# The first feed-forward product of blocks two to four by seven products, its weight sums made in block one, and the last norm off VectorE

## The chip, the cores and the metric

The kernel runs on one core of a Trainium2 chip. A core has five engines that run their own instruction streams: TensorE (PE, matmul, with a separate weight load), VectorE (DVE), ScalarE (ACT), GpSimd (POOL) and SyncE (SP), which here only issues DMAs. The metric is the device time of one execution in microseconds (us); it was measured three times for the kernel before.

## The reference

One decoder layer in fp32 over 2048 tokens of width 1024: a gated DeltaNet mixer of 8 heads and a memory cross-attention of 4 heads share one input projection and one output projection; then a post-norm, a feed-forward network and a second post-norm. The part that the change touches:

```python
D_MODEL = 1024; SEQ = 2048; D_FF = 4 * D_MODEL; ALPHA = 2.0 ** 0.25
def layer_norm(x, g, b):
    mu = x.mean(-1, keepdims=True)
    var = jnp.square(x - mu).mean(-1, keepdims=True)
    return (x - mu) * lax.rsqrt(var + LN_EPS) * g + b
def sqrelu_mlp(x, w1, w2):
    return jnp.square(jax.nn.relu(x @ w1)) @ w2
...
mix = gdn_mixer(x, mem_k, mem_v, ...)
x = layer_norm(ALPHA * x + mix, ln1_g, ln1_b)
x = layer_norm(ALPHA * x + sqrelu_mlp(x, w_ff1, w_ff2), ln2_g, ln2_b)
```

## The kernel before

**Blocks and stages.** The 2048 tokens run in four blocks of 512 (`TB`), one after the other; the recurrent state is carried between them. In a block follow: input projections (`aq`, `ak`, `av`, `az`), the gates and the chunked delta rule by heads, the output projection (`ao`, summed into the token tiles `y`, 128 tokens by 1024 each), norm 1, the two feed-forward products (FF1 and FF2, both in PSUM banks named `af` in the profile), norm 2 and the store.

**Precision.** Each fp32 operand is split into a high part (an ACT cast) and a low part (a DVE subtraction), and `mm3` (L475) makes each product by three matmuls: high x high, high x low, low x high. For a weight tile of 128x1024 this is one DMA into `wraw`, one cast and one subtraction into a `whl` pair. There are `NW` = 4 `whl` pairs and `NR` = 3 `wraw` buffers (L387). The transposed tokens after norm 1 lie in `Thi` and `Tlo`, made by `to_T` (L535): eight transposes of 128x128 per token tile into `pt` and two splits.

**FF1** (`ff1_tiles`, L1213) makes one 128-feature tile by 512 tokens with `project` (L548): 8 contraction tiles of 128, 24 matmuls of 512 columns. The first four tiles of a block run in two token halves of 256 columns instead, so that PE can begin before the last token tiles are through norm 1. `relu2` (L1208) squares the positive part on ACT.

**FF2** (`ff_seven`, L1011) runs in 4 groups `g` of 1024 features, each of two parts `v`. It uses the Winograd form of Strassen's product: seven products of halves in place of eight, with sums `S1` to `S4` of the left operand (`ss4` tiles on DVE, from the squares `sq2`; both show as `ss` and `sq`) and sums of the weights, which `keep_sums` (L991) makes on DVE in block 1 and stores in DRAM as `tsc`. The table `SEVEN` lists the products and the banks that they are added into.

**Last norm.** `layer_norm` (L512) takes statistics and their aggregate on DVE (`bn`, `mv`), two tiny POOL steps (`ve`, `rs`), and then per half of 512 columns two DVE steps with g and b; norm 2 of a block runs in the middle of FF2's last group and behind it, together with the first projections and the gates (`gab`, `gp`, `gg`, then `pg`, `pgt` on PE) of the next block, which `next_block` (L1115) sets in between.

**Order.** No engine's order is written by hand. Every operation is recorded, and `Recorder.issue` simulates the five engines with a cost per operation (`cost`), latencies and buffer releases, and takes on each engine the ready operation of the smallest recorded index plus `nc.shift`. The resulting order is fixed at build time; the hardware then only waits by semaphores. All instructions are issued at L330, so in the profile one goes by the tiles' names. All DMAs stand in SP's queue, in order.

Of the kernel before, what the change touches and what calls it, by code (L numbers as in the profile page):

```python
# [14 lines left out]
P = 128  # L15
TB = 512
# [330 lines left out]
def hybrid_layer(  # L347
# [102 lines left out]
    inv = {}  # L450
    for n, f in (("LB", P), ("XB", P), ("L32", P), ("X32", P), ("X64", P), ("L64", P), ("Q", 64)):
        inv[n] = rec.buf(cst, (P, 2, f), F32, n, 1, n)
        nc.gpsimd.memset(inv[n], 0.0)
# [58 lines left out]
    def layer_norm(y, g, b, dst=None):  # L512
        st = small("bn", [P, 2, BN_DIM])
        for i in range(2):
            nc.vector.bn_stats(out=st[:, i], in_=y[:, i * 512:(i + 1) * 512].part(i))
        mv = small("mv", [P, 2])
        nc.vector.bn_aggr(out=mv, in_=st)
        ve = small("ve", [P, 1])
        nc.gpsimd.tensor_scalar_add(ve, mv[:, 1:2], LN_EPS)
        rs = small("rs", [P, 1])  # L520
        nc.gpsimd.tensor_tensor(out=rs, in0=ve, in1=mhalf[:, 0:1], op=ALU.pow)
        for i in range(2):
            c = slice(i * 512, (i + 1) * 512)
            yi = y[:, c].part(i)
            nc.vector.scalar_tensor_tensor(out=yi, in0=yi, scalar=mv[:, 0:1], in1=g[:, c],
                                           op0=ALU.subtract, op1=ALU.mult)
# [17 lines left out]
    def T_tiles():  # L544
        return (rec.buf(tp, (P, KT, TB), F32R, "Thi", 1, "Thi"),
                rec.buf(tp, (P, KT, TB), F32R, "Tlo", 1, "Tlo"))

# [458 lines left out]

    SEVEN = (("A11", "B11", "A", False, (0, 0)), ("S3", 3, "C", False, (1, 1)), ("S2", 2, "A", True, (1, 0)),
# [3 lines left out]
    def ff_seven(b, ff1_tiles, relu2, add, norm2):  # L1011
        Q = 2 * P
        for g in range(NS):
# [3 lines left out]
            for v in range(2):  # L1017
                lo = [slot("xl", "s%d" % v, F32R) for _ in range(7)]
                hi = [slot("xh", "d", F32R) for _ in range(7 if v == 0 else 4)]
                if v:  # L1020
                    hi += [hq[:, 0].part(0), hq[:, 1].part(1), slot("xh", "on", F32R)]
                sqs = [None, None]
                fs = [8 * g + 2 * v + o for o in (0, 4, 1, 5)]
                for part in ((0, 1, 2, 3),) if g == 0 and v == 0 else ((0,), (1,), (2,), (3,)):
                    if b == 0:
                        for j in range(2):
                            if 2 * j in part:
                                keep_sums(u0 + v, j)
                    for i, a in zip(part, ff1_tiles([fs[i] for i in part], len(part) > 1)):
# [7 lines left out]
                        st = tok_tile("ss4")  # L1037
                        a11, a21, a12, a22 = (sq[:, q * Q:(q + 1) * Q] for q in range(4))
                        s = [st[:, q * Q:(q + 1) * Q].part(q // 2) for q in range(4)]
                        sub = lambda o, x, y, op=ALU.subtract: nc.vector.tensor_tensor(out=o, in0=x, in1=y, op=op)  # L1040
                        sub(s[0], a21, a22, ALU.add)
                        sub(s[1], s[0], a11)
                        sub(s[2], a11, a21)
                        sub(s[3], a12, s[1])
                        h3, l3 = hi[3 * j:3 * j + 3], lo[3 * j:3 * j + 3]
                        two = lambda ap: ap.rearrange("p (i f) -> p i f", i=2)
                        split(sq.rearrange("p (j i f) -> p i j f", j=2, i=2)[:, 0], two(h3[0]), two(l3[0]))
                        h22 = hi[6][:, j * Q:(j + 1) * Q].part(("x", j))
                        l22 = lo[6][:, j * Q:(j + 1) * Q].part(j)
                        split(a22, h22, l22)  # L1050
                        for q in range(2):
                            split(st[:, q * TB:(q + 1) * TB].part(q), h3[1 + q], l3[1 + q])
                        x = {"A22": (h22, l22)}
                        for q, (n0, n1) in enumerate((("A11", "A12"), ("S1", "S2"), ("S3", "S4"))):
                            x[n0] = h3[q][:, :Q], l3[q][:, :Q]
                            x[n1] = h3[q][:, Q:], l3[q][:, Q:]
                        X[2 * v + j] = x
# [57 lines left out]
    def next_block(b, step):  # L1115
# [3 lines left out]
        if step < 4:  # L1119
# [3 lines left out]
            xj = rec.buf(wp, (P, 1024), F32, "wraw", NR, "xj").rearrange("p (k f) -> p k f", k=2)  # L1123
# [8 lines left out]
    for b in range(NB):  # L1132
# [12 lines left out]
        for i in range(12):  # L1145
            cat_slot(i)
        r, A = {}, {}
# [14 lines left out]
        def out_proj(k0, tail=None):  # L1162
# [28 lines left out]
            else:  # L1191
                for t in range(NC):
# [8 lines left out]
        T1 = T_tiles()  # L1201

        def norm1(t):
            layer_norm(ys[t], g1, b1)
            to_T(ys[t], T1[0], T1[1], t)

# [6 lines left out]
        def ff1_tiles(fs, halves):  # L1213

            wa = [(load_cols(w_ff1, f), bank("af", "m" if halves and i == 3 else "acc")) for i, f in enumerate(fs)]
            for t0, n in ((0, 256), (256, 256)) if halves else ((0, TB),):
                for w, a in wa:
                    project(a[:, t0:t0 + n], w, T1, n, t0)
            return [a for _, a in wa]

# [12 lines left out]
        ff_seven(b, ff1_tiles, relu2, add, norm2)  # L1233
# [56 lines left out]
```

## Time and profile before

| what | value |
|---|---|
| time, median of 3 runs | 2924.38 us (2924.02 to 2924.44) |
| the profiled execution | 2924.22 us |
| its span | 2922.5 us |
| mean granted TensorE clock | 0.994 of full speed |
| PE, DVE, ACT, POOL busy in the feed-forward of block 2 (301 us) | 300.0, 184.3, 148.8, 2.0 us |
| the same at the transition to block 3 (46 us) | 42.2, 40.6, 15.7, 9.5 us |

The span is the profiler's, from the first to the last instruction; the time holds a little more. In the profile a row of a group reads: engine, operation, output and inputs, shapes, count, then busy us and mean ns of one, then the idle time just ahead of such instructions and what ended it. In a timeline a row begins with start and length in us; a wait stands in brackets with its releaser. Matmuls overlap, so the pace of a row of matmuls, not the length of one, is what it costs.

### The profile page before, as it was taken

The numbers are of one execution on the slowest core, as the hardware profiler recorded it, in microseconds if no ns is written. First come the engines' busy times: TensorE is split into PE (matmuls) and PEld (weight loads), VectorE is DVE, ScalarE is ACT, GpSimd is POOL, SyncE is SP. The second block draws the span as 40 slices with busy tenths as digits, with TensorE's granted clock in tenths as the row PEclk, the third lists the DMA queues.
The fourth block names the chain that finished last, engine by engine and source line by source line (L and its number), as shares of the span: only waits on it lengthen the run. The fifth ranks groups of instructions, "written<-read, shape, count | busy, mean of one in ns | idle before, by whom it ended". The sixth has DMA issues, their size and how long they took to land.

```text
span 2922.5 us, 42803 instructions
## 1 busy us (share of the span) xinstructions
PE 2863.8 (98%) x14404; PEld 2387.9 (82%) x14404; DVE 2182.8 (75%) x5762; ACT 1528.2 (52%) x3678; POOL 419.6 (14%) x1033
## 2 busy tenths in 40 slices
PE   8999999999999999999999999999999999999998
PEld 6888778888788888888878888888877888888886
DVE  7999987666788886665578887756667888676667
ACT  6677625554356652555436665344454666444443
POOL 1334200000123311000013331100002223010000
PEclk9999999999999999999999999999999999999999
DMA  7755567655743322544474333244446332324444
GB/s 254 271 202 202 175 207 249 204 188 187 265 166 127 125 96 80 159 139 136 151 261 146 138 109 105 87 151 144 151 161 245 139 139 95 104 94 147 149 144 137
DMA packets 127708, 469.79 MB, mean 161 GB/s; under 512 B 14464, under 2 KB 16896, under 8 KB 109056
## 3 DMA queue, kind: packets, MB, share of 16 engines
q1 hardware_dynamic: 126912, 467.00, 47.6%
q8 instruction: 114, 1.87, 0.3%
q14 instruction: 106, 0.87, 0.1%
q10 hardware_dynamic: 576, 0.06, 0.0%
HBM read 402.97 MB, written 64.03 MB: 160 GB/s over the span
## 4 chain that ended last, share of the span: by engine, by line
PE 84%; DVE 12%; issue 1%; POOL 1%; ACT 1%; DMA 0%; POOLq 0%; ACTq 0%; DVEq 0%
PE af L330 43%; PE ao L330 7%; PE aq L330 5%; PE az L330 4%; PE ak L330 4%; PE av L330 4%; PE pc L330 3%; PE amq L330 3%; DVE y L330 3%; PE po L330 2%; PE pkq L330 1%; PE pq L330 1%; PE pp L330 1%; DVE bn L330 1%; DVE whl L330 1%
## 5 line engine op out<-in xcount | busy, mean ns | idle before, releaser
L330 DVE TENSOR_TENSOR whl<-wraw,whl 128x1024 fp32r<-128x1024 f32 (+1 forms) x446 | 540.1, 1217 | 424.2 <-ACT whl L330 414.9
L330 PE MATMUL af<-Thi,whl 128*128 128x512 f32 (+1 forms) x2304 | 650.7, 367 | 7.0 <-DVE whl L330 6.4
L330 ACT CAST whl<-wraw 128x1024 fp32r<-128x1024 f32 (+1 forms) x446 | 466.4, 1047 | 359.8 <-PE af L330 196.2
L330 PEld LDWEIGHTS af<-Thi,whl 128*128 128x128 f32 x2304 | 417.7, 189 | 78.5 <-DVE whl L330 7.2
L330 PE MATMUL af<-whl,xh 128*128 128x512 f32 x1536 | 473.6, 390 | 3.1 <-DVE whl L330 3.1
L330 PE MATMUL af<-Tlo,whl 128*128 128x512 f32 (+1 forms) x1152 | 422.0, 366 | 0.0
L330 PE MATMUL af<-whl,xl 128*128 128x512 f32 x896 | 346.1, 389 | 0.0
L330 PEld LDWEIGHTS af<-whl,xh 128*128 128x128 f32 x1536 | 287.7, 188 | 66.5 <-DVE whl L330 5.0
L330 PE MATMUL ao<-whl,ch 128*128 128x512 f32 x768 | 254.2, 402 | 2.0 <-DVE y L330 1.6
L330 PEld LDWEIGHTS af<-Tlo,whl 128*128 128x128 f32 x1152 | 217.9, 189 | 34.9
L330 POOL TENSOR_SCALAR ve<-mv 128x1 f32<-128x1 f32 x34 | 24.9, 731 | 1512.7 <-DVE mv L330 1487.1
L330 ACT ACTIVATE rl<-af 128x512 f32<-128x512 f32 x128 | 76.5, 598 | 274.0 <-PE af L330 272.1
L330 PEld LDWEIGHTS af<-whl,xl 128*128 128x128 f32 x896 | 168.2, 188 | 34.9
L330 PE MATMUL aq<-Thi,whl 128*128 128x512 f32 x512 | 179.5, 410 | 8.4 <-ACT Thi L330 6.9
L330 PE MATMUL av<-Thi,whl 128*128 128x512 f32 x512 | 181.2, 413 | 0.0
L330 DVE SCALAR_TENSOR_TENSOR y<-y,af 128x512 f32<-128x512 f32 x224 | 148.8, 683 | 43.2 <-PE af L330 43.2
L330 PE MATMUL ak<-Thi,whl 128*128 128x512 f32 x512 | 173.7, 402 | 0.0
L330 PE MATMUL az<-Thi,whl 128*128 128x512 f32 x512 | 171.8, 401 | 0.1
L330 PEld LDWEIGHTS ao<-whl,ch 128*128 128x128 f32 x768 | 142.5, 188 | 28.6 <-DVE y L330 2.9
L330 PE MATMUL ao<-whl,cl 128*128 128x512 f32 x384 | 152.3, 399 | 0.0
L330 PEld LDWEIGHTS aq<-Thi,whl 128*128 128x128 f32 x512 | 95.4, 191 | 24.4 <-ACT Thi L330 6.9
L330 PEld LDWEIGHTS av<-Thi,whl 128*128 128x128 f32 x512 | 97.7, 195 | 16.5
(257 smaller groups left out, 5812.8 us busy)
## 6 DMA issues: line engine op xcount, KB each, us to landing
wraw<-in_w_ff_dram SPq DMA_DIRECT2D x224, 512.0 KB, 4.1
whl<-wsc SPq DMA_DIRECT2D x108, 1024.0 KB, 4.9
wraw<-tsc SPq DMA_DIRECT2D x128, 512.0 KB, 3.4
wsc<-whl SPq DMA_DIRECT2D x36, 1024.0 KB, 5.6
wraw<-in_w_out_dram SPq DMA_DIRECT2D x48, 512.0 KB, 3.9
wraw<-in_w_in_dram SPq DMA_DIRECT2D x35, 512.0 KB, 6.5
wq<-in_w_ff_dram SPq DMA_DIRECT2D x64, 256.0 KB, 4.4
tsc<-wq SPq DMA_DIRECT2D x64, 256.0 KB, 3.8
```

The source lines that it names most:

```text
L330: o.fn(*[res(a) for a in o.args], **{k: res(v) for k, v in o.kw.items()})
```

## The change

1. FF1 of blocks 2 to 4 is made by seven products as well: the contraction (1024) is halved, the 256-feature output and the 512 tokens are halved, and each product is 24 matmuls of 256 columns for each of two 128-feature tiles (`FF1_SEVEN`, `ff1_quads`). Block 1 keeps `ff1_tiles`.
2. The weight sums `S1` to `S4` that this needs are made by POOL in block 1 from the raw FF1 weights (`ff1_sums`) and stored in DRAM as `fsc`: 128 sums and 128 stores of 128x256. The raw weights keep their `wraw` buffers until then.
3. The transposed tokens are kept as quadrants (`quad_tiles`, `to_quads`): four plain or summed quadrants in `Thi`/`Tlo`, the sums T1, T2, T4 in other tiles' places, T1 in a `whl` pair. The token tiles go through the last output projection in the order 2, 3, 0, 1, since the sums need both halves of the tokens.
4. Reading the results: ACT copies and squares of 256 columns, DVE sums from PSUM, and the FF2 sums `ss4` of blocks 2 to 4 on POOL. `put` splits smaller pieces.
5. Norm 2 of blocks 1 to 3 is "light": one ACT step and two POOL steps per half instead of two DVE steps.
6. Room: the inverse's tiles move to a shared pool `inv` and are cleared anew in each block; the next block's x (`xj`) uses one buffer `kq1` instead of a `wraw`.

Instructions that differ (before, after): matmuls into FF banks of 512 columns from FF1 2688, 672, of 256 columns 768, 4224; weights cast and split 443, 515; POOL rows 1038, 1463; SP rows 870, 1070. The diff, cut to its core:

```diff
-    def layer_norm(y, g, b, dst=None):
+    def layer_norm(y, g, b, dst=None, light=False):
...
+            if light:
+                nc.scalar.activation(yi, yi, AF.Identity, bias=nm, scale=rs)
+                nc.gpsimd.tensor_tensor(out=yi, in0=yi, in1=g[:, c], op=ALU.mult)
+                nc.gpsimd.tensor_tensor(out=yi, in0=yi, in1=b[:, c], op=ALU.add)
+                nc.sync.dma_start(out=dst[:, c], in_=yi)
+                continue
...
+    def to_quads(y, Q, keep, t):
+        pts = []
+        for j in range(2):
+            pt = bank("pt", ("ga0", "ga1", "m")[(2 * t + j) % 3])
+            for k in range(4):
+                nc.tensor.transpose(pt[:, k * P:(k + 1) * P], y[:, (4 * j + k) * P:(4 * j + k + 1) * P].part(j), ident)
+            pts.append(v4(pt))
+            if t >= 2:
+                quad_split(Q, ("B11", "B21")[j], t, pts[j])
+                f = v4(slot("tf", "d"))
+                nc.scalar.copy(out=f, in_=pts[j])
+                keep[t, j] = f
+        if t < 2:
+            nc.shift = 200 if t == 0 else 130
...
+            if t == 0:
+                b12, eng, b22 = s["B12"], nc.gpsimd, v4(slot("tf", "d"))
+                nc.scalar.copy(out=b22, in_=pts[1])
+            sub(s["T1"], b12, keep[t + 2, 0])
+            sub(s["T2"], b22, s["T1"])
+            sub(s["T3"], b22, s["B12"])
+            eng = nc.gpsimd
+            sub(s["T4"], keep[t + 2, 1], s["T2"])
+            quad_split(Q, "T2", t, s["T2"])
+            quad_split(Q, "T3", t, s["T3"])
+            quad_split(Q, "B22", t, b22)
+            quad_split(Q, "T1", t, s["T1"])
+            quad_split(Q, "T4", t, s["T4"])
+            nc.shift = 0
...
+    FF1_SEVEN = (("A11", "B11", "A", False), ("A12", "B21", "B", False), ("S2", "T2", "A", True), ("S3", "T3", "C", False),
+                 ("S1", "T1", "A", True), ("A22", "T4", "C", True), ("S4", "B22", "A", True))
...
+    def ff1_sums(f):
...
+        for i in range(2):
...
+                nc.gpsimd.tensor_tensor(out=s[n], in0=x, in1=y, op=op)
+                nc.sync.dma_start(out=fsc[v, n][:, 512 * j + 256 * i:512 * j + 256 * i + 256].part(2 * j + i), in_=s[n])
...
-            xj = rec.buf(wp, (P, 1024), F32, "wraw", NR, "xj").rearrange("p (k f) -> p k f", k=2)
+            xj = rec.buf(tp, (P, 2, TB), F32, "kq1", 1, "xj")
...
-                for t in range(NC):
+                for t in (2, 3, 0, 1) if b else range(NC):
...
+        def ff1_quads(vs, ACs, Bs, put):
...
+                    for k in range(4):
+                        th, tl = quad_k(T1, tn, k)
+                        for m, (a, x) in enumerate(((hi, th), (hi, tl), (lo, th))):
...
+            def read(v, n, i, o):
...
+                sub = lambda o, x, y, op=ALU.subtract: nc.gpsimd.tensor_tensor(out=o, in0=x, in1=y, op=op)
+                if wn in ("A11", "S2", "S3"):
+                    nc.scalar.copy(out=sq({"A11": 3, "S2": 1, "S3": 0}[wn]), in_=o)
+                    return
+                q = {"A12": 3, "S1": 0, "A22": 1, "S4": 2}[wn]
+                if wn == "S4":
+                    nc.scalar.activation(sq(q), o, AF.Relu)
+                else:
+                    nc.vector.tensor_tensor(out=sq(q), in0=sq(q), in1=o, op=ALU.add)
+                    nc.scalar.activation(sq(q), sq(q), AF.Relu)
+                nc.scalar.activation(sq(q), sq(q), AF.Square)
...
-                layer_norm(ys[t], gb[0], gb[1], od[b * NC + t])
+                layer_norm(ys[t], gb[0], gb[1], od[b * NC + t], b < NB - 1)
```

How the order moves, at three places. First POOL at norm 1 of block 2. Before, its rows there are only `ve` and `rs`, a pair for each token tile. Now (`tq` and `tf` are tiles of the token sums and of kept transposes, `mv` a tile's statistics):

```order
L330 TENSOR_SCALAR ve_12957<-mv_12951 128x1
L330 TENSOR_TENSOR rs_12963<-ve_12957,mhalf_101 128x1
L330 TENSOR_TENSOR tq_13007<-tq_12998,tf_12852 128x512
L330 TENSOR_TENSOR tq_13028<-tf_13010,tq_12998 128x512
L330 TENSOR_TENSOR tq_13039<-tf_13010,tq_13007 128x512
L330 TENSOR_SCALAR ve_13055<-mv_13047 128x1
L330 TENSOR_TENSOR tq_13061<-tf_12864,tq_13039 128x512
L330 TENSOR_TENSOR rs_13077<-ve_13055,mhalf_101 128x1
```

Three subtractions of 512 columns stand ahead of the last tile's `ve`, and a fourth between it and `rs`. Second, DVE behind that `rs`, before, from the last scaling to the third weight behind it:

```order
L330 SCALAR_TENSOR_TENSOR y_12034<-y_12034,rs_12546,l1b_12092 128x512 x2
L330 TENSOR_TENSOR whl_12525<-wraw_12474,whl_12525 128x1024
L330 TENSOR_TENSOR Tlo_12374<-pt_12577,Thi_12362 128x4x128
L330 TENSOR_TENSOR Tlo_12374<-pt_12585,Thi_12362 128x4x128
L330 TENSOR_TENSOR whl_12666<-wraw_12539,whl_12666 128x1024
L330 TENSOR_TENSOR whl_12699<-wraw_12556,whl_12699 128x1024
```

and now, from the same scaling on:

```order
L330 SCALAR_TENSOR_TENSOR y_12271<-y_12271,rs_13077,l1b_12580 128x512 x2
L330 TENSOR_TENSOR Tx_13105<-tq_13039,Tx_13059 128x128
L330 TENSOR_TENSOR whl_13092<-wraw_13034,whl_13092 128x1024
L330 TENSOR_TENSOR tq_13123<-pt_13099,tf_12918 128x512
L330 TENSOR_TENSOR Tlo_12860<-pt_13109,Thi_12846 128x4x128
L330 TENSOR_TENSOR tq_13139<-pt_13109,tq_13123 128x512
...
L330 TENSOR_TENSOR Tx_13220<-tq_13061,Tx_13080 128x2x128
L330 TENSOR_TENSOR Tx_13225<-tq_13061,Tx_13085 128x2x128
L330 TENSOR_TENSOR whl_13142<-wraw_13051,whl_13142 128x1024
L330 TENSOR_TENSOR whl_13195<-wraw_13070,whl_13195 128x1024
```

Between S2's weight (`whl_13092`) and S3's (`whl_13142`) stand 22 steps that form token sums and their low parts, where before there were two. Third, SP in block 1, before, in FF1's first group:

```order
L330 DMA wraw_5042<-in_w_ff1_dram 128x1024
L330 DMA wraw_5054<-in_w_ff1_dram 128x1024
L330 DMA tsc_4318<-wq_4973 128x512
L330 DMA tsc_4352<-wq_4973 128x512
L330 DMA tsc_5079<-wq_4967 128x512
```

and now:

```order
L330 DMA wraw_5042<-in_w_ff1_dram 128x1024
L330 DMA fsc_5053<-fs_5044 128x256
L330 DMA fsc_5053<-fs_5050 128x256
L330 DMA wraw_5063<-in_w_ff1_dram 128x1024
L330 DMA tsc_4318<-wq_4973 128x512
L330 DMA tsc_4352<-wq_4973 128x512
```

The stores of the FF1 sums (`fsc`) now stand between the loads of the weights, each waiting for its POOL step.

More of the change, by code (lines that the diff above doesn't have):

```diff
@@ L1146, in hybrid_layer @@
             cat_slot(i)
+        inverse_tiles()
         r, A = {}, {}
@@ L1213, in ff1_tiles @@
         def ff1_tiles(fs, halves):
-            wa = [(load_cols(w_ff1, f), bank("af", "m" if halves and i == 3 else "acc")) for i, f in enumerate(fs)]
+            wa = []
+            for i, f in enumerate(fs):
+                rt = rec.buf(wp, (P, 1024), F32, "wraw", NR, "wraw")
+                nc.sync.dma_start(out=rt, in_=w_ff1[f])
+                wa.append((as_cols(*hilo(rt)[1:]), bank("af", "m" if halves and i == 3 else "acc")))
+                raws[f] = rt
             for t0, n in ((0, 256), (256, 256)) if halves else ((0, TB),):
```

210 lines of the change are left out of this document (181 added, 29 removed).

## The prediction

> **What bounds the kernel now.** First the page: busy time by engine, and the shares of the chain of work that ended last.
>
> ```profile
> PE 2863.8 (98%) x14404; PEld 2387.9 (82%) x14404; DVE 2182.8 (75%) x5762; ACT 1528.2 (52%) x3678; POOL 419.6 (14%) x1033
> PE 84%; DVE 12%; issue 1%; POOL 1%; ACT 1%; DMA 0%; POOLq 0%; ACTq 0%; DVEq 0%
> PE af L330 43%; PE ao L330 7%; PE aq L330 5%; PE az L330 4%; PE ak L330 4%; PE av L330 4%; PE pc L330 3%; PE amq L330 3%; DVE y L330 3%; PE po L330 2%; PE pkq L330 1%; PE pq L330 1%; PE pp L330 1%; DVE bn L330 1%; DVE whl L330 1%
> ```
>
> TensorE (PE) is busy for 2863.8 of 2922.5 us, and `af`, the feed-forward products, are 43% of the chain: matmuls that leave the program are worth their time, if nobody else becomes the bound where they go. Second, the windows by stage: feed-forward of block 1 and of block 2, the out projection with norm 1 ahead of block 2's feed-forward, the transition to block 3 and two pieces of it. Columns: window, length, busy time of PE, weight load, VectorE (DVE), ScalarE (ACT), GpSimd (POOL), then the granted clock, DMA share, GB/s.
>
> ```profile
> 432.00:739.00 307.00, 304.88 (x1428) 255.79 (x1429) 210.11 (x302) 149.71 (x209) 2.00 (x2) 0.99 0.62 205
> 1153.00:1454.00 301.00, 300.02 (x1404) 251.54 (x1405) 184.33 (x262) 148.83 (x208) 2.01 (x2) 1.00 0.46 142
> 1083.00:1153.00 70.00, 69.40 (x350) 57.04 (x348) 49.85 (x79) 23.48 (x44) 7.59 (x9) 1.00 0.32 98
> 1454.00:1500.00 46.00, 42.16 (x186) 32.98 (x185) 40.62 (x82) 15.70 (x23) 9.48 (x15) 0.97 0.87 295
> 1496.00:1500.00 4.00, 1.34 (x6) 1.24 (x7) 4.00 (x12) 2.17 (x6) 2.53 (x4) 0.69 0.98 363
> 1500.00:1504.00 4.00, 4.00 (x10) 3.05 (x10) 3.13 (x6) 0.83 (x3) 0.00 (x0) 0.50 0.99 401
> ```
>
> Inside a feed-forward stage PE is the bound: 300.0 of 301 us, while DVE has 117 us to spare, ACT 152 and POOL 299. At the transition DVE is busy 40.6 of 46 us and PE idles 3.8. Third, what PE waited for in the whole run (total, times, longest), and the two waits at that transition.
>
> ```profile
> PE af L330 <- DVE whl L330: 9.5, 8, 3.0
> PE pg L330 <- DVE gg L330: 6.0, 3, 2.0
> PE pgt L330 <- DVE gkd L330: 4.3, 3, 1.5
> 1497.37 0.47 PE L330 MATMUL pg<-gg,triu 128*128 128x32 f32 x2 [2.01 <-DVE gg L330]
> 1499.56 0.40 PE L330 MATMUL pgt<-ident,gc 128*32 128x128 f32 x1 [1.30 <-DVE gkd L330]
> ```
>
> So PE's few waits are on DVE, at the two ends of the feed-forward.
>
> **The matmuls: -42 us.** The counts of 512-wide and 256-wide products, the pace of 256-wide ones in PE's timeline, and one 512-wide run in the chain.
>
> ```profile
> L330 PE MATMUL af<-Thi,whl 128*128 128x512 f32 x1792 | 554.2, 389 | 0.0
> L330 PE MATMUL af<-Thi,whl 128*128 128x256 f32 x512 | 97.1, 288 | 7.0 <-DVE whl L330 6.4 <-DVE Tlo L330 0.6
> 1160.58 0.40 PE L330 MATMUL af<-Thi,whl 128*128 128x256 f32 x2
> 1160.82 0.28 PE L330 MATMUL af<-Tlo,whl 128*128 128x256 f32 x1
> 1160.94 0.40 PE L330 MATMUL af<-Thi,whl 128*128 128x256 f32 x2
> 81.79 5.44 PE av L330 x24
> ```
>
> Two of every three products have the high tokens, so the first form is 1792 x 1.5 = 2688 in four blocks, 672 each, and the second 192 each. Means of one overlap; the pace is what counts: 24 wide ones in 5.44 us are 0.2267 us each, and three narrow ones from 1160.58 to 1160.94 are 0.120 us each. FF1 of a block is now 672 x 0.2267 + 192 x 0.120 = 175.4 us. By seven products it is 4 groups x 2 pairs x 7 products x 2 row halves x 4 k x 3 = 1344 narrow ones, 161.3 us. That is -14.1 us a block, -42.3 for three (an eighth fewer products would give -22; narrow matmuls cost 6% more per column).
>
> **Norm 1 and the start of FF1: +16, and +3 for the clock.** The chain through norm 1 of block 2, then the PE wait that ends it and a transpose.
>
> ```profile
> 1138.45 0.80 POOL ve L330
> 1139.32 0.94 POOL rs L330
> 1140.28 2.61 DVE y L330 x4
> 1142.89 1.20 DVE Tlo L330 x2
> 1144.09 1.19 DVE bn L330 x2
> 1146.08 1.09 DVE whl L330
> 1153.98 0.51 PE L330 MATMUL af<-Thi,whl 128*128 128x256 f32 x2 [1.16 <-DVE whl L330]
> 1157.49 0.44 PE pt L330 x4
> ```
>
> Here DVE paces PE already: the wait costs 1.16 us, with 0.19 more just before. Back to back a DVE step takes 0.65 us (y), 0.60 (split of 512, statistics) or 1.09 to 1.13 (split of a weight). In the new order DVE must finish before the weight of S3: four token tiles at 2 sums, 2 statistics, 1 aggregate and 4 scalings (5.1 us each, 20.4); the first two tiles' low parts, 2.4; three subtractions that form T1 to T3 of the second pair, 1.8; the low parts of six quadrants, many as pieces of 128 columns, 6.5; six weights, 6.8; two sums from PSUM, 0.7. That is 38.6 us. POOL's `ve` and `rs` (0.80 + 0.94) now stand behind four POOL subtractions of 512, (8 us, of which three run while DVE is busy elsewhere); I take 5 us of waits: 43.6. PE has, from the first sum on, seven out-projection products of 2.72 us (19.0), four weights of 24 narrow matmuls (11.5), S2's weight (2.9) and eight transposes of 0.44 (3.5): 36.9. The stall is 6.7 instead of 1.35 us, +5.3 a block, +16. Bounds: 0 (POOL early) to +10 a block (each subtraction at its locked price, below). After 3.3 us of waits at the transition above the clock was 0.50 for 4 us, which loses 2 us; a stall of 6.7 us may do so too, or come in pieces: I take +1 a block, +3. The Trainium skill, TensorE: Matmul & The Clock Gate, "Why this matters for your kernels", tells to leave no idle gap above about 3 us, or the clock halves; rows 0.69 and 0.50 agree, and by it this term would be +6.
>
> **Inside FF1: +6.** Two weight casts of FF2 on ACT, then groups: DVE's sums, the last norm's scalings, and a POOL step of 256 columns with one input.
>
> ```profile
> 1218.13 1.05 ACT L330 CAST whl<-wraw 128x1024 fp32r<-128x1024 f32 x1 [1.67 <-PE af L330]
> 1220.85 1.05 ACT L330 CAST whl<-wraw 128x1024 fp32r<-128x1024 f32 x1 [1.67 <-PE af L330]
> L330 DVE TENSOR_TENSOR ss<-sq 128x256 f32<-128x256 f32 x128 | 48.3, 419 | 0.0
> L330 DVE SCALAR_TENSOR_TENSOR y<-y,mv,l2g 128x512 f32<-128x512 f32 x32 | 23.1, 748 | 0.0
> L330 POOL TENSOR_SCALAR L<-dl 64x256 f32<-64x256 f32 x32 | 33.6, 1050 | 40.9 <-PE pq L330 27.9 <-PE pmT L330 9.0 <-DVE Bc L330 2.9
> ```
>
> FF1 now takes 7 weights where it took 4, one for every 24 x 0.120 = 2.88 us of PE. FF2 already lives on one weight per 2.72 us, with ACT waiting for PE, so 72 more weights (casts, splits, loads of 512 KB) lie beside PE. Per pair (20.2 us of PE) DVE has some 14 us, ACT 17, POOL eight sums of 256. No row shows a two-input sum on POOL; the nearest are DVE's 0.42 us and POOL's one-input step of the same width, 1.05 in the mean. I take 1.0, because it is the same engine. These sums are queued in order with the reads of PSUM: if one is late, ACT and DVE wait, and PE for a bank. One of the four weight pairs is taken by T1 until its product ends, so the lead is some 3.4 us. I take +0.5 us a group, +6; bounds 0 and +15.
>
> **Block 1: +4.** 16 pairs of raw weights give eight POOL sums each (128) and 128 stores. First a load and a store of SP's queue (size, median us to landing), then one POOL step twice, with the DVE steps beside it.
>
> ```profile
> wraw<-in_w_ff_dram SPq DMA_DIRECT2D x224, 512.0 KB, 4.1
> tsc<-wq SPq DMA_DIRECT2D x64, 256.0 KB, 3.8
> 296.60 1.88 POOL L330 TENSOR_SCALAR L<-dl 64x256 f32<-64x256 f32 x1 [2.80 <-PE pq L330]
> 919.94 0.86 POOL L330 TENSOR_SCALAR L<-dl 64x256 f32<-64x256 f32 x1 [1.74 <-PE pq L330]
> 296.54 1.22 DVE L330 TENSOR_TENSOR whl<-wraw,whl 128x1024 fp32r<-128x1024 f32 x1
> 920.05 0.34 DVE L330 TENSOR_TENSOR Bc<-Bc,Lc 128x32 f32<-128x32 f32 x1
> 920.42 0.19 DVE L330 TENSOR_TENSOR Xc<-Xc,Bc 128x32 f32<-128x32 f32 x1
> ```
>
> 128 us of POOL fit into a stage where it has 305 idle. But a raw pair keeps its buffers until its sums are made: 8 x 1.05 + 4.1 for the load is 12.5 us, PE needs 10.9 for the two products; 1.6 us x 16 pairs = 26 is the upper bound, 0 the lower, since FF2 (168 products of 0.2267, 38 us a group) lets the loads run ahead again. A store in SP's queue stands before the next load, but lands beside it. I take +4. The same POOL step takes 0.86 us alone and 1.88 when it starts inside a 1.22 us DVE subtraction with two inputs; a DVE step that starts inside it takes 0.34 instead of 0.19. The two engines hold each other up. The Trainium skill, GPSIMD Engine Reference, section 1, says that both share their SBUF interfaces and collide where DVE reads two SBUF inputs, which these rows show. Its section 3.1 gives a two-input sum on POOL 1.96 times DVE's time; as an estimate that is 0.82 us for 256 columns, 10.7 us a pair, and block 1 would then cost nothing.
>
> **Transitions: -7.** The last norm of blocks 1 to 3 loses 16 scalings on DVE each (at 0.67, 10.7 us) to ACT and POOL; the gate chain up to `gg` stands less mixed with y work, and PE has matmuls behind it. The waits `pg` and `pgt` total 10.3 us and each pair costs 2 at half clock: -16 if all goes. Against it POOL has two sums of 512 per half (16 a block, some 2 us each by twice the 256 value) before the stores, which sit in SP's queue ahead of weight loads, and xj now has one buffer, so its four loads follow each other. Bounds -16 to +6; I take -7.
>
> **Sum.** -42.3 + 16 + 3 + 6 + 4 - 7 = -20, from the profiled execution's 2924.22 us, 0.16 below the median of 2924.38: 2904.
>
> **Rivals.**
> A, all is hidden: the stall at norm 1 stays as it was and the transitions gain: 2924 - 42 = 2882, down to 2875. For: PE 300 of 301 with three engines half free. Against: DVE full at norm 1 (above).
> B, the gain is given back in block 1 and behind SP's queue: +26 for the raw pairs instead of +4: 2926, no change. For: one PE engine bound to three raw buffers. Against: SP's loads have a share of 0.62 and FF2 gives slack.
> C, slower: POOL's wide two-input steps hold DVE. There are 128 of 256 columns in block 1 and in each later block 64 of 256, 16 + 5 of 512. A DVE step was held 0.15 us by the one-input step above, and at most such a step's whole 0.86: I take 0.5 us for 256 columns and two inputs, between the two, and 1.0 for 512: 64 + 3 x 53 = 223 us. Where DVE has slack this is nothing; the stages at norm 1 and transitions have none. With the other terms as they are, it is slower once 26 us of these, 12%, reach PE beyond what the terms count; at a fifth, 2904 + 45 - 10 that the terms hold already = 2939.
> D, narrow matmuls do not keep 0.120 us when their weights change from quadrant to quadrant: at 0.133, 4032 x 0.013 = +52, slower too, 2956; the rows above keep 0.120 from one weight to the next, so hardly.
>
> **Chances.** Forecast (2890 to 2918) 0.44; A 0.20; B 0.17; C 0.16; D 0.03. 0.2% is about 6 us, what a measurement tells from no change: faster holds the forecast, A and a little of B, 0.68; same 0.12; slower C, D and B's upper end, 0.20. Range 2880 to 2934; the likeliest case's own is 2890 to 2918.
>
> **What would show it.** FF1 of blocks 2 to 4 at 161 us by narrow `af` at 0.120; a PE wait of 5 to 8 us on `whl` or `Tx` at each norm 1, with a low clock behind; `pg` and `pgt` waits gone; POOL steps of 256 near 1 us; block 1 within 5 us of 307. Wrong if PE waits on weights inside FF1, if block 1 grows by over 10 us, or if DVE's splits lengthen beside POOL.

## The result and the profile after

The changed kernel takes 3019.26 us (3018.21 to 3022.32, 4 runs) against 2924.41 for the kernel before (2924.02 to 2927.52, 4 runs): ratio 1.0324, 95% interval 1.0306 to 1.0342. It is 95 us slower, where 20 us faster was forecast.

The page's busy times of the changed kernel, then the spans with the mean granted clock of the changed kernel and of the one before:

```profile
PE 2870.4 (95%) x15844; PEld 2439.6 (81%) x15844; DVE 2388.9 (79%) x5853; ACT 1703.7 (56%) x4219; POOL 863.5 (29%) x1458
```

```profile
core 0: 3020.6 us, clock 0.987
```

```profile
core 0: 2922.5 us, clock 0.994
```

TensorE has 42 us of matmuls less and yet 2870.4 us of busy time, where it had 2863.8. A row of 24 narrow matmuls that stands between waits shows 3.22 us where their pace gives 2.88 (below), and a lower clock stretches matmuls: as an estimate from spans and clocks, 0.013 x 3020.6 - 0.006 x 2922.5 = 22 us more than before were lost by the clock. What it waited for (total us, times, longest):

```profile
PE af L330 <- DVE whl L330: 40.7, 27, 3.3
PE af L330 <- ACT sq L330: 31.1, 25, 3.5
PE af L330 <- ACT whl L330: 12.1, 11, 2.2
PE pt L330 <- DVE y L330: 10.6, 10, 2.3
```

Before, `af` waited 9.5 us for DVE's `whl` and not at all for `sq` or for ACT. Where it happens is read from block 3, stage by stage (windows; the columns are those of the prediction). The changed kernel: the first FF1 group, its FF2, the second FF1 group, its FF2, the FF2 of the third group, the last FF2 with the transition.

```profile
1904.30:1966.00 61.70, 48.62 (x353) 45.44 (x352) 48.98 (x72) 39.55 (x82) 20.66 (x16) 0.94 0.39 128
1966.00:2005.40 39.40, 38.43 (x171) 31.48 (x170) 30.39 (x35) 18.59 (x26) 7.99 (x8) 1.00 0.59 186
2005.40:2048.80 43.40, 41.36 (x337) 40.51 (x336) 29.44 (x39) 32.01 (x67) 10.04 (x10) 1.00 0.53 171
2048.80:2091.40 42.60, 40.36 (x171) 32.59 (x171) 31.66 (x36) 18.65 (x26) 7.45 (x7) 0.96 0.54 172
2134.90:2175.80 40.90, 38.66 (x170) 31.35 (x169) 31.47 (x36) 18.57 (x26) 7.38 (x7) 1.00 0.58 179
2219.30:2273.40 54.10, 47.08 (x195) 35.60 (x194) 44.63 (x57) 24.71 (x34) 22.38 (x25) 0.96 0.74 251
```

The kernel before: first FF1 group, its FF2, second FF1 group, last FF2 with the transition.

```profile
1863.80:1912.20 48.40, 47.05 (x306) 42.91 (x305) 31.26 (x50) 23.76 (x38) 2.46 (x3) 1.00 0.37 119
1912.20:1950.20 38.00, 38.00 (x169) 31.49 (x168) 27.70 (x35) 17.75 (x20) 0.00 (x0) 1.00 0.57 180
1950.20:1993.80 43.60, 43.60 (x194) 36.08 (x194) 21.30 (x34) 22.01 (x34) 0.00 (x0) 1.00 0.36 110
2157.00:2204.70 47.70, 47.17 (x209) 36.95 (x208) 40.84 (x67) 19.49 (x24) 4.04 (x7) 1.00 0.72 240
```

So the first FF1 group loses 13.3 us, the three later ones take 43.4 instead of the 40.3 that their 336 matmuls need and gain nothing, FF2 (its matmuls unchanged) loses 1.4, 4.5 and 2.8 us behind them, and the end 6.4: 28 of the 29 us that block 3 became longer. The later FF1 groups take 43.4 or 43.5 us in all three blocks.

The rows of PE at four of these waits:

```profile
1917.52 0.66 PE L330 MATMUL pt<-ident,y 128*128 128x128 f32 x4 [2.29 <-DVE y L330]
1950.93 0.63 PE L330 MATMUL af<-Tx,whl 128*128 128x256 f32 x2 [3.50 <-ACT sq L330]
2033.49 3.22 PE L330 MATMUL af<-Tx,whl 128*128 128x256 f32 x24 [1.65 <-ACT sq L330]
2060.19 0.65 PE L330 MATMUL af<-whl,xh 128*128 128x512 f32 x1 [2.12 <-DVE whl L330]
```

The first is answered below, and the last is a weight of FF2 that comes late. The second and third are new, waits for a bank. In the seven-product form a bank is read between accumulations, and the next product may not add to it before ACT has copied it (`sq<-af`). The ACT rows just ahead of the 3.50 us show why that copy came late:

```profile
1945.34 0.62 ACT L330 CAST xh<-ss 128x512 fp32r<-128x512 f32 x1 [1.34 <-POOL ss L330]
1948.24 0.62 ACT L330 CAST xh<-ss 128x512 fp32r<-128x512 f32 x1 [0.45 <-POOL ss L330]
1949.90 0.40 ACT L330 CAST xh<-ss 128x256 fp32r<-128x256 f32 x1 [1.04 <-POOL ss L330]
1950.53 0.35 ACT L330 COPY sq<-af 128x256 f32<-128x256 f32 x1
```

ACT's queue is in order: casts of FF2's sums stand ahead of the copy, and wait for POOL. POOL's sums at that place, and DVE's rows beside and behind them:

```profile
1943.52 1.79 POOL L330 TENSOR_TENSOR ss<-ss,sq 128x256 f32<-128x256 f32 x1
1945.27 2.07 POOL L330 TENSOR_TENSOR ss<-sq 128x256 f32<-128x256 f32 x2
1948.16 1.70 POOL L330 TENSOR_TENSOR ss<-sq,ss 128x256 f32<-128x256 f32 x1
```

```profile
1949.21 1.88 DVE L330 TENSOR_TENSOR xl<-ss,xh 128x256 fp32r<-128x256 f32 x3
1954.09 0.42 DVE L330 TENSOR_TENSOR xl<-ss,xh 128x256 fp32r<-128x256 f32 x1
```

A sum takes 1.0 to 1.8 us, and DVE's split of 256 columns 0.63 us beside them, 0.42 without.

At norm 1 of the same block POOL holds two token sums in 4.49 us, then `ve` and `rs` behind a further one; a weight split beside them takes 2.18 us (1.22 before), and PE's transposes wait 2.29 us for `y`:

```profile
1908.33 4.49 POOL L330 TENSOR_TENSOR tq<-tf,tq 128x512 f32<-128x512 f32 x2
1912.79 1.19 POOL L330 TENSOR_SCALAR ve<-mv 128x1 f32<-128x1 f32 x1
1915.66 1.01 POOL L330 TENSOR_TENSOR rs<-ve,mhalf 128x1 f32<-128x1 f32 x1
```

```profile
1911.72 2.18 DVE L330 TENSOR_TENSOR whl<-wraw,whl 128x1024 fp32r<-128x1024 f32 x1
```

### The profile page after: what moved, and what is told of

The parts are those of the page before. It is cut to its first block, busy times and chain, and to the rows that moved or that the text cites. A ratio compares the mean times of both kernels' runs of the same rounds, so it can differ in the third digit from the quotient of the medians.

```text
span 3020.6 us, 47476 instructions
## 1 busy us (share of the span) xinstructions
PE 2870.4 (95%) x15844; PEld 2439.6 (81%) x15844; DVE 2388.9 (79%) x5853; ACT 1703.7 (56%) x4219; POOL 863.5 (29%) x1458
## 5 line engine op out<-in xcount | busy, mean ns | idle before, releaser
L330 DVE TENSOR_TENSOR whl<-wraw,whl 128x1024 fp32r<-128x1024 f32 (+1 forms) x518 | 656.9, 1274 | 238.0 <-ACT whl L330 233.6
L330 ACT CAST whl<-wraw 128x1024 fp32r<-128x1024 f32 (+1 forms) x518 | 540.2, 1047 | 420.9 <-PE af L330 216.2
L330 PE MATMUL af<-whl,xh 128*128 128x512 f32 x1536 | 489.2, 396 | 40.5 <-DVE whl L330 31.6
L330 PE MATMUL af<-Thi,whl 128*128 128x256 f32 (+1 forms) x2112 | 456.9, 309 | 17.0 <-DVE whl L330 9.1
L330 PEld LDWEIGHTS af<-whl,xh 128*128 128x128 f32 x1536 | 290.6, 190 | 115.2 <-DVE whl L330 43.4
L330 PEld LDWEIGHTS af<-Thi,whl 128*128 128x128 f32 x2112 | 349.8, 192 | 41.0 <-DVE whl L330 11.1
L330 PE MATMUL af<-Tlo,whl 128*128 128x256 f32 (+1 forms) x1056 | 323.8, 307 | 4.3 <-ACT sq L330 2.8
L330 POOL TENSOR_TENSOR ss<-sq 128x256 f32<-128x256 f32 x96 | 92.5, 982 | 684.4 <-ACT sq L330 621.9
L330 PE MATMUL af<-Tx,whl 128*128 128x256 f32 x1728 | 228.2, 289 | 31.1 <-ACT sq L330 28.1
L330 PEld LDWEIGHTS af<-Tx,whl 128*128 128x128 f32 x1728 | 216.5, 195 | 39.5 <-ACT sq L330 31.9
L330 ACT ACTIVATE sq<-sq 128x256 f32<-128x256 f32 x336 | 124.9, 410 | 11.5 <-DVE sq L330 9.6
```

The costliest lines, as they stand in the source:

```text
L330: o.fn(*[res(a) for a in o.args], **{k: res(v) for k, v in o.kw.items()})
```

## The experiments

Each edit takes one cause away or puts it back, and some runs join several. All but the three that say so were timed once; the kernel before gave 2924 to 2931 us beside them, so differences under some 5 us between two of these runs say nothing. The runs without T1, token sums or operand sums leave out terms that the product needs: they price these terms and are no kernels to use. The theories named are L (POOL and DVE hold each other up), W (too much work, or one weight pair too few), P (the planner's price of POOL), Q (ACT's queue behind POOL's sums) and N (token sums at norm 1).

**POOL's work back to DVE, one part at a time.**

```diff
# e_ss_dve, in read()
-                sub = lambda ...: nc.gpsimd.tensor_tensor(...)
+                sub = lambda ...: nc.vector.tensor_tensor(...)
# e_norm_dve, in norm2()
-                layer_norm(ys[t], gb[0], gb[1], od[b * NC + t], b < NB - 1)
+                layer_norm(ys[t], gb[0], gb[1], od[b * NC + t])
# e_tq_dve, in to_quads()
-                b12, eng, b22 = s["B12"], nc.gpsimd, v4(slot("tf", "d"))
+                b12, eng, b22 = s["B12"], nc.vector, v4(slot("tf", "d"))
...
-            eng = nc.gpsimd
```

> The FF2 operand sums ss4 of blocks 2 to 4 (192 steps of 128x256) go from POOL back to DVE; all else as changed. Theory L (POOL's wide two-input steps and DVE's hold each other up, and ACT and DVE, whose queues are in order, wait behind the late sums until PE lacks a weight or a bank): the losses of the three later FF1 groups and of FF2 behind them (18 us a block) go, and a part of the first group's 16: 3019 - 3 x (18 + 5) = about 2950 us; DVE's weight split back to 1.22 us inside FF1, PE's waits on ACT sq below 8 us in all. Theory W (DVE and ACT simply have too much to do, or one weight pair too few with T1 in it): DVE gets 192 x 0.335 = 64 us more, PE waits as before or longer: 3019 to 3060 us.

> The last norm of blocks 1 to 3 is made on DVE again (no light norm); all else as changed. Theory L: the transitions lose 6 to 7 us each by POOL's 16 steps of 512 beside DVE's splits; without them 3019 - 3 x 6 = about 3000 us, and the stage of 54 us back to 48. Theory W: DVE is the bound there too, 16 scalings more cost 0 to 10 us a block: 3019 to 3050 us.

> The token sums of norm 1 (five of 512 columns a block) go from POOL to DVE; all else as changed. Theory L: rs no longer waits behind them and two weight splits of 1.70 and 2.18 us fall to 1.22; PE's wait of 2.3 us for y at the last tile goes: 3 to 6 us a block, about 3005 us. Theory W: five DVE steps of 0.6 us more a block on a full DVE: 3019 + 9 = about 3028 us.

> All three of the above: sums ss4, last norm and token sums on DVE; on POOL only block one's weight sums remain beside what was there before the change. Theory L: the gain of the matmuls comes back but for what the start of FF1 costs by DVE's own work: about 2915 us, between 2890 and 2940. Theory W: above 3019 us.

Measured: 2996.1, 3005.9, 3012.8 and, all three together, 2988.5 us. Each helps, by 23, 13 and 6.5 us, but together by 31 only, and 64 us above the kernel before stay. L alone does not hold: it asked for about 2950 and 2915 us in the first and the last. That the parts do not add fits a share of W, the work that comes back to DVE, but these four do not show it apart.

**The planner's price, the pair, and the parts alone in the kernel before.**

```diff
# e_cost, in Recorder.cost()
-        return 150 + 2.1 * n if name == "tensor_tensor" else 176 + 1.3 * n
+        return 150 + 3.2 * n if name == "tensor_tensor" else 176 + 1.3 * n
# e_no_t1, in quad_tiles(); quad_split(Q, "T1", ...) goes, and quad_k reads "B22" for "T1"
-        t = rec.buf(wp, (P, 2, 4, 256), F32R, "whl", NW, "Tx")
-        Q["T1"] = [[t[:, i]] for i in range(2)]
+        Q["T1"] = Q["B22"]
# e_before_hold, in the kernel before: written at norm1(2), read after the last FF1 product
+        hold = rec.buf(wp, (P, 2 * 1024), F32R, "whl", NW, "hold") if b else None
# e_before_ss_pool, in the kernel before, in ff_seven()
-                        sub = lambda ...: nc.vector.tensor_tensor(...)
+                        sub = lambda ...: (nc.gpsimd if b else nc.vector).tensor_tensor(...)
```

> The changed kernel with one number of its planner changed: a two-input POOL step of n columns is priced at 150 + 3.2 n ns (969 for 256, 1788 for 512) in place of 150 + 2.1 n (688 and 1225); the rows of the changed kernel show 982 ns for 256. The same work, another order. Theory P (the order of ACT and DVE was laid out for POOL sums that come 0.3 us earlier than they do, so that queues which are in order wait on them and PE behind these): a third to two thirds of the 141 us lost return, 2925 to 2970 us, and ACT's waits for POOL ss in FF1 shrink. Theory L (the two engines hold each other up whatever the order): 3010 to 3030 us. Theory W (one weight pair too few, with T1 in it): 3010 to 3025 us.

> S1's product takes B22's quadrant in place of T1, which is not split or kept; so all four weight pairs serve weights in blocks 2 to 4, with the same number of matmuls. Theory W: the stalls on whl at the start of FF2 (2 us and the clock behind it) and in FF1 go: 5 to 12 us a block, 2983 to 3004 us. Theories L and P: within 6 us of 3019, but for the four splits less at norm 1 (1 to 2 us a block), so 3010 to 3019 us.

> The kernel before, in which one of the four weight pairs is held, unused, from norm 1 to the last FF1 product of blocks 2 to 4, as T1 holds it in the change. Theory W: FF2's three first groups of 38.1 us grow by 1 to 4 each: 2924 + 3 x 3 x 2.5 = 2946 us or so. Theories L and P: the pair is no bound by itself, 2924 to 2930 us.

> The kernel before, in which only the FF2 operand sums of blocks 2 to 4 go to POOL (192 steps of 128x256, as in the change). Theory L: POOL holds DVE here too; the weight splits beside them lengthen from 1.22 to 1.7 us, and PE waits 1 to 3 us in each of 12 groups: 2936 to 2960 us. Theory P: FF1 by full products leaves 2.7 us per weight on ACT, so that a sum that comes late is covered: 2920 to 2928 us. Theory W: as before, 2924 or a little less.

Measured: 3008.2, 2982.9, 2927.2 and 2922.2 us. A truer price gives 11 us, less than P asked for. Without T1 36 us return, the most that W named. FF2 of the second group and the end are then (windows of that run):

```profile
2033.30:2071.80 38.50, 38.45 (x171) 31.51 (x170) 31.43 (x36) 18.64 (x26) 7.43 (x7) 1.00 0.58 190
2197.20:2243.60 46.40, 44.53 (x196) 34.43 (x195) 39.62 (x51) 22.48 (x31) 18.69 (x21) 1.00 0.70 240
```

38.5 instead of 42.6 and 46.4 instead of 54.1; its later FF1 groups stay at 43.4. But the same pair held in the kernel before costs nothing, and POOL's sums in the kernel before cost nothing either. The latter was timed again, 11 times:

> The kernel before with only the FF2 sums of blocks 2 to 4 on POOL, timed in five rounds. One look gave 2922.2 us beside 2928.7 for the kernel before, which elsewhere took 2924.4. If the part gains by itself (DVE freed, FF1's lead is long): 0.998 to 0.9995 of the kernel before. If it was the run: 1.000 within the interval.

The ratio is 0.9982, interval 0.9973 to 0.9991: a little faster. Yet the groups of instructions (busy us, mean ns) show DVE's splits of 256 columns twice as long as in the kernel before, first that kernel, then this run:

```profile
L330 DVE TENSOR_TENSOR xl<-sq,xh 128x256 fp32r<-128x256 f32 x64 | 27.0, 421 | 0.0
```

```profile
L330 DVE TENSOR_TENSOR xl<-sq,xh 128x256 fp32r<-128x256 f32 x64 | 52.5, 820 | 0.0
```

And POOL's sums are no faster there than in the change, first this run, then the changed kernel:

```profile
L330 POOL TENSOR_TENSOR ss<-sq 128x256 f32<-128x256 f32 x96 | 116.0, 1227 | 669.0 <-ACT sq L330 666.4 <-DMA wraw<-in_w_ff_dram 2.7
L330 POOL TENSOR_TENSOR ss<-ss,sq 128x256 f32<-128x256 f32 x48 | 44.7, 930 | 0.0
```

```profile
L330 POOL TENSOR_TENSOR ss<-sq 128x256 f32<-128x256 f32 x96 | 92.5, 982 | 684.4 <-ACT sq L330 621.9 <-DVE whl L330 42.2 <-issue 20.3
L330 POOL TENSOR_TENSOR ss<-sq,ss 128x256 f32<-128x256 f32 x48 | 61.1, 1287 | 4.5 <-ACT sq L330 4.5
```

So the two engines do hold each other up, and that is free in this kernel, where an FF1 weight lasts 5.44 us and no FF1 bank is read between accumulations; which of the two matters is not shown apart. Theory Q came from this: what counts is what stands behind the late sum.

**The causes taken away one after the other.** Without T1 the sums ss4 are left out, or put on DVE; then the token sums; then both.

```diff
# e_t1_no_ss = e_no_t1 and, in read():
-                    sub(ss(0), sq(1), sq(3), ALU.add)
-                    sub(ss(2), sq(0), sq(1))
-                    sub(ss(1), ss(0), sq(0))
-                    put(v, i, ("S3",), st[:, 2:3].part(2))
+                    put(v, i, ("S3",), a[:, 0:1].part(0))
...
# e_t1_ss_dve = e_no_t1 and e_ss_dve
# e_no_tq, in to_quads(), and quad_k reads B22, B21, B22 for T1, T2, T4
-            sub(s["T1"], b12, keep[t + 2, 0])
...
-            quad_split(Q, "T4", t, s["T4"])
+            quad_split(Q, "T3", t, b12)
+            quad_split(Q, "B22", t, b22)
# e_bare = e_t1_no_ss and e_no_tq
```

> S1's product takes B22 in place of T1 (no T1, four weight pairs), and FF2's operand sums ss4 of blocks 2 to 4 are left out on every engine: the casts read the squares themselves. To be read against the run without T1 alone (2983 us). Theory Q (what is left of FF1's loss is ACT's queue: casts of xh wait for POOL's sums, the reads of PSUM behind them come late, PE waits for the bank): FF1's later groups go from 43.5 to about 40.5 us, 3 x 3 x 3 = 27 us and some in the first group: 2945 to 2955 us. Theory W (too much work on DVE and ACT as such; the sums are on neither): within 8 us of 2983.

> As the run without T1 (four weight pairs), with the sums ss4 on DVE in place of POOL. Theory Q: ACT no longer waits for POOL; with four pairs DVE's 8 sums more per pair of products (2.7 us of 20.2) are covered, FF1's later groups at 40.5 to 41.5 us: 2950 to 2960 us. Theory W: DVE is the bound, groups stay at 43.5 to 44: 2980 to 3000 us.

> The token sums T1 to T4 are left out: their products take the plain quadrants, with as many matmuls; no POOL or DVE subtraction, no split of T1, T2 and T4 at norm 1, and four weight pairs. Against 2983 us without T1 alone it shows what the token sums cost at norm 1. Theory N (the start of FF1 is lost to the token sums and their 22 DVE steps): the first FF1 group falls from 58 to 60 us to 47 to 49, 2983 - 3 x 11 = 2950 us. If the order of the token tiles and the narrow start do it instead: 2975 to 2983 us.

> Both left out, the token sums and the sums ss4: seven narrow products, their weights and the reads remain, with block one's weight sums and the light norm. If the three causes (pair, POOL sums in ACT's queue, token sums at norm 1) are the whole loss but for transitions and block one, FF1 takes 40.4 us a group, 46 the first, FF2 38.1: 2924 - 42 + 6 (block one) + 3 x 7 (transitions) = about 2910 us. Theory W: 2940 us or more, FF1's groups above 42 us.

Measured: 2954.7, 2956.6, 2959.4 and 2921.2 us. The sums on DVE or on no engine at all give the same, 28 us (left out) and 26 us (on DVE) below the run without T1, and with the sums on DVE PE's waits for ACT's `sq` fall from 29.0 to 3.0 us: it was not the work of the sums but their place in the queues. That is Q; how much later the sums come because DVE holds POOL is not shown apart. The token sums cost 24 us beside POOL's sums (2982.9 to 2959.4) and 34 without them (2954.7 to 2921.2), where N asked for 33. Beside POOL's sums the first group of block 3 still takes 52.9 us (58.3 with the token sums), not the 47 to 49 that N named; without both it takes 46.6. The bare run's 2921.2 us is 11 above what was expected, and its later FF1 groups are above 42 us, a sign that was named for W. Its second group of block 3, then the same group with all its sums and without T1 (e_t1_ss_dve), then the bare run's two longest waits by kind:

```profile
1953.90:1996.20 42.30, 41.08 (x338) 40.48 (x337) 27.15 (x42) 32.48 (x71) 0.00 (x0) 1.00 0.48 164
```

```profile
1978.30:2019.40 41.10, 40.85 (x338) 40.44 (x337) 30.26 (x51) 32.15 (x68) 0.00 (x0) 1.00 0.49 169
```

```profile
PE af L330 <- DVE sq L330: 14.5, 27, 0.6
PE pg L330 <- DVE gg L330: 11.7, 3, 4.8
```

Bare, a group takes 42.3 and not 40.3 us, with 27 waits of 0.5 us for DVE's sum from a bank that the next product adds to. They do not lie in the form of the seven products alone: with more work for DVE but another order the group takes 41.1 us, and PE waits for `sq` only 5.5 us in that whole run. Nor is one cause enough by itself: without T1 but with POOL's sums the later groups stay at 43.4, with T1 and the sums on DVE (e_ss_dve) at 43.7, and only without both they fall.

**The light norm, block one and the moved tiles.**

```diff
# e_bare_norm = e_bare and e_norm_dve
# e_classic: FF1 of all blocks by ff1_tiles, to_T and the old token order; light norm and block one's sums stay
-        T1 = quad_tiles() if b else T_tiles()
+        T1 = T_tiles()
...
# e_classic_norm = e_classic and e_norm_dve
# e_best = e_classic_norm without ff1_sums
# e_best_ss = e_best with ss4 of blocks 2 to 4 on POOL
```

> As the run with token sums and FF2 sums left out (2921 us), and the last norm of blocks 1 to 3 on DVE again. If the light norm's POOL steps make the gates late on DVE (PE's wait of 4.8 us for gg), 3 x 5 us or so return: about 2905 us, pg's waits back near 2 us. If the transition is bound by DVE's own work, 2921 to 2930 us.

> The changed kernel with FF1 of all blocks by full products, as before, the token tiles transposed as before and in the old order, and ss4 on DVE; what remains of the change are block one's weight sums on POOL, the light norm, the smaller splits and the moved tiles. If these cost what the stage times of the changed kernel show (block one +6, transitions +5 each): 2924 + 6 + 15 = 2945 us. If they cost only together with the narrow products: 2922 to 2930 us.

> The same with the last norm on DVE in all blocks. What it lies above the kernel before is block one's sums and the moved tiles, about 2930 us; what it lies below the run with the light norm is the light norm, 15 us; 0 if the light norm costs nothing by itself.

> Of the change only the moved tiles and the smaller splits remain: xj in its own buffer, inverse tiles in a shared pool, pieces of X split one by one; FF1 by full products, no weight sums in block one, last norm on DVE. If xj out of wraw is what gained: 0.995 to 0.998 of the kernel before, about 2915 us; if the 2918 us before was the run: 0.999 to 1.001.

> The same with the FF2 sums of blocks 2 to 4 on POOL. If both gains add: 2 to 6 us below the run without them, about 0.995; if POOL's sums only gained by the order they gave: equal to it within 2 us.

Measured, the first three: 2907.1, 2934.4 and 2918.2 us. The light norm costs 14 us in the bare kernel and 16 in the classic one. It does not lose them in the last FF2: in block 3 that takes 43.3 us with it and 44.3 without (e_classic, e_classic_norm), but from there to the next FF1 it takes 381 us instead of 372. The changed kernel's trace at the end of block 3 shows what becomes late. A gate step of 32 columns beside POOL's sums for the norm takes 1.22 us. And a copy that the convolution needs stands behind such sums in POOL's queue, and DVE waits for it; this second wait is not shown to reach PE, which goes on there. First the changed kernel's POOL, then its DVE, then the same gate step in the kernel before, 0.18 us.

```profile
2264.43 2.54 POOL L330 TENSOR_TENSOR y<-y,l2b 128x512 f32<-128x512 f32 x2
2286.59 2.53 POOL L330 TENSOR_TENSOR y<-y,l2b 128x512 f32<-128x512 f32 x2
2289.06 0.31 POOL L330 COPY raw<-halo 128x3 f32<-128x3 f32 x2
```

```profile
2265.80 1.22 DVE L330 SCALAR_TENSOR_TENSOR gt<-gy 128x32 f32<-128x32 f32 x1
2289.28 0.75 DVE L330 SCALAR_TENSOR_TENSOR cq<-raw,cw,cq 128x512 f32<-128x512 f32 x1 [7.43 <-POOL raw L330]
```

```profile
1485.32 0.18 DVE L330 SCALAR_TENSOR_TENSOR gt<-gy 128x32 f32<-128x32 f32 x1
```

What reaches PE is the wait for the gates, here in the classic run with the light norm; it was 6.0 us in the kernel before and is gone in e_classic_norm and e_best:

```profile
PE pg L330 <- DVE gg L330: 13.3, 3, 5.5
```

The last two, timed five times each: e_best takes 2906.81 us, ratio 0.9931 (0.9916 to 0.9945), and e_best_ss 2910.58, 0.9947 (0.9934 to 0.9960). The gain of POOL's sums in the kernel before does not add here. e_best is 0.7% faster than the kernel before; it keeps only the moved tiles and the finer splits with their order. Its feed-forward of block 1 and its last FF2 with the transition of block 3, then block 1 with the weight sums (e_classic_norm):

```profile
430.30:771.90 341.60, 338.16 (x1580) 281.52 (x1579) 246.04 (x376) 164.03 (x241) 5.81 (x8) 1.00 0.64 213
2148.40:2192.50 44.10, 44.10 (x197) 34.77 (x196) 40.30 (x67) 19.48 (x25) 4.02 (x7) 1.00 0.74 254
```

```profile
431.10:781.00 349.90, 340.72 (x1580) 282.94 (x1579) 279.81 (x377) 166.92 (x241) 136.29 (x133) 0.99 0.78 253
```

The transition is 44.1 instead of 47.7 us with no PE idle, and block 1 341.6 instead of 346.5; the weight sums cost 8.3 us there. Which of xj's own buffer, the shared pool and the finer splits gives the gain was not tried apart.

## Why the prediction was wrong

**The ledger.** 3019.3 (all) to 2982.9 without T1, its splits and its pair (36), to 2954.7 without POOL's sums in ACT's queue (28), to 2921.2 without the token sums (34), to 2907.1 without the light norm (14). The runs without T1 are incomplete products, and each figure depends on what was already gone: 23 us for POOL's sums with T1 in place, 28 without it. Of the 39 us between the profiled spans with and without T1, some 25 lie in FF2 behind the first three groups of each block, where no T1 is split, 6 in the first groups and the rest in and behind the last FF2: so the pair held seems to count for more than the splits. At that point full products take 2918.2 with the same block one and norm: seven narrow products, without any of their sums, are worth 11 us there, not 42, and without block one's sums full products take 2906.8. Most of what was forecast to gain is used up even there. By stages the profiled execution is 98 us longer: 85 in the feed-forward stages of blocks 2 to 4, 2 in that of block 1, and 10 ahead of the feed-forward of blocks 1 and 2, whose cause was not sought.

**The matmuls: -42 forecast, count and pace right.** A product has 24 narrow matmuls in all, 12 for each of its two feature tiles, and not 24 for each as the description of the change reads. 24 of them in 3.22 us with the tail of the last one (2033.49) fit 0.120 each. But the term took it that PE would stay busy; the reads between accumulations cost up to 2 us in each of nine later groups in the bare run (18 us), and 0.8 us in the best order seen.

**Inside FF1: +6 forecast, the step that failed.** "72 more weights lie beside PE" and "+0.5 us a group" were drawn from the busy time of engines. In the trace the later FF1 groups lose 3.1 us each against 40.3 (28 us in nine) and FF2 behind the first three groups 8.7 us in block 3 and some 10 in blocks 2 and 4 (29): 57 us. I had named the wait ("if one is late, ACT and DVE wait, and PE for a bank") and priced it at a sixth of what a group lost (0.5 against 3.1 us; single waits took 3.50 and 1.65), because what stands behind a late sum is a whole queue, and because the pair that T1 holds leaves no lead to absorb it.

**Norm 1 and the start: +16 and +3 forecast, mis-sized.** The first group lost 13.3 us and the 4.5 that its matmuls were to gain (192 x 0.120 + 96 x 0.2267 = 44.8 to 40.3), 17.8 in block 3 and some 52 in all, where 6.3 a block stood in the sum. The stall is not one of 6.7 us ahead of S3's weight but 14 shorter ones, 13.1 us in all, of which 2.29 us for the late `y` and 3.50 for a bank are the longest; the POOL subtractions ahead of `rs` were seen, but priced without what they do to DVE's splits. The clock behind these waits is in these figures: 0.94 in the first group of block 3.

**Block 1: +4 forecast.** The stage grew by 2.0 us; apart, the weight sums cost 8.3 and the moved tiles give some 5 back. The term was right in sign, and the raw pairs (B) did not decide the result.

**Transitions: -7 forecast, wrong way.** The stage grew by 6.4 us in block 3, for the most part by T1's pair: the last FF2 of block 4, which has neither a light norm nor a transition, grew as much, and without T1 the stage of block 3 takes 46.4 us, 1.3 less than before. That FF2 in the changed kernel, and in the kernel before:

```profile
2964.30:3020.60 56.30, 40.89 (x170) 32.06 (x168) 46.15 (x63) 16.55 (x24) 12.66 (x15) 0.90 0.44 150
```

```profile
2872.70:2922.50 49.80, 38.24 (x169) 31.34 (x167) 40.77 (x61) 14.59 (x17) 5.29 (x8) 0.92 0.38 129
```

Besides, two parts of opposite sign were put together: the moved tiles and finer splits do gain (20 us in e_best, over the whole run), the light norm loses 14, at the start of the next block. The gain was ascribed to the norm's steps leaving DVE; what POOL's steps do to the gates on DVE beside them was left out.

**The rivals.** C was on the right side and named POOL's two-input steps, but DVE held by POOL is not by itself what costs inside FF1: with 192 such steps and splits of 0.82 us the kernel before did not become slower. A and B are out by the result, D by the pace of 0.120 us that was kept. Of the signs that were named, DVE's longer splits and PE's waits inside FF1 came, for banks more than for weights. The Trainium skill, GPSIMD Engine Reference, section 3.1, has a two-input sum on POOL at 1.96 times DVE's time, from which 0.82 us was estimated for 256 columns; the means measured are 0.93 to 1.29 us in the two kernels, and the measurement decides. That DVE's work beside them makes the difference is likely but not shown.

## What to carry to other kernels

Fewer matmuls help only as long as each result can be read before the next product adds to its bank; count for each bank how long the reader has, and what stands ahead of it in its queue. Two causes can hide each other, as T1's pair and POOL's sums did: where taking one away changes nothing at a place, take both. An idle engine is not free room: work that is moved there is paid by what waits behind its results in the in-order queues of others, so follow the moved step's consumers and its own queue, not its busy time. And measure the side moves of a change alone: here the moved tiles and finer splits by themselves made the faster kernel.

## What was not expected of the hardware

A wait of 2.12 us could be enough for the clock: behind it (2060.19) a 512-wide matmul shows 0.65 us, where the mean of one was 389 ns in the kernel before, and the granted clock of the 5 us behind it is 0.66. But 86 us later a wait of 2.10 us for the same weight of the next group is followed by a clock of 1.00:

```profile
2060.20:2065.20 5.00, 5.00 (x15) 3.96 (x16) 3.58 (x4) 0.78 (x1) 0.00 (x0) 0.66 0.71 236
2146.20:2151.20 5.00, 4.98 (x22) 4.13 (x23) 4.02 (x5) 1.05 (x1) 0.00 (x0) 1.00 0.74 210
```

Of the seven waits of 2.10 to 2.12 us at this place in the three blocks, five are followed by 0.66 or 0.67 and two by 1.00, while none of the nine gaps of 1.65 us for `sq`, as at 2033.49, is followed by less than 1.00. So the length of a gap alone does not decide; what else does is not shown. The Trainium skill, TensorE: Matmul & The Clock Gate, "Why this matters for your kernels", speaks of gaps above about 3 us; here less was enough, five times of seven. And a DVE step of 32 columns, 0.18 us by itself, took 1.22 us beside POOL's 512-column sums, so even a small step on a critical chain can be held by wide ones on the other engine.
